# Encoder kernel, Fourier branch of the mixer: the second weight granule formed directly behind the first, ahead of the masked products; the maxima of one half moved behind exponentials

## The chip, the cores and the metric

One core of a Trainium2 chip runs the whole kernel in one launch. The metric is the device time of one execution in microseconds, the median of several runs; lower is better. The engines of the core are named as in the profile: PE (matrix products), PEld (its weight loads), DVE (vector engine), ACT (scalar engine), POOL and SP (here mainly queues that issue DMAs).

## The reference

Two layers of an encoder on 512 tokens of width 1024, in float32. The part that matters is the mixer of each layer:

```python
for l in range(DEPTH):                       # DEPTH = 2
    x = x + 0.5 * swiglu(rms_norm(x, ffn1_norm[l]), ffn1_w_in[l], ffn1_w_out[l])
    x = x + mixer(rms_norm(x, mix_norm[l]), ...)
    x = x + 0.5 * swiglu(rms_norm(x, ffn2_norm[l]), ffn2_w_in[l], ffn2_w_out[l])
return rms_norm(x, final_norm)

def mixer(h, w_in, gate_bias, rpb, w_na_out, w_f_out, w_o):
    z = h @ w_in                             # q, k, v, uf, ga, gf are column blocks of z
    y_na = neighbourhood_attention(q, k, v, rpb) @ w_na_out
    y_f = fourier_mix(uf) @ w_f_out          # real part of a 2-D DFT per channel group
    return (sigmoid(ga + gate_bias[0]) * y_na + sigmoid(gf + gate_bias[1]) * y_f) @ w_o

def neighbourhood_attention(q, k, v, rpb):   # 8 heads of 64, 2-D windows with a learned bias
    s = q k^T * scale + bias, masked outside the window
    return softmax(s) v
```

## The kernel before

**Precision.** A float32 product is made of three PE passes over operands that are each split into a rounded high part and a low rest: high by high, low by high, high by low (`mm3`, lines 316 to 318). So each operand that reaches PE is first split: ACT copies the high part, then DVE subtracts it from the source and writes the low part.

**Weights.** All weights lie in DRAM as granules of 128 x 1024 numbers, in the order of use. `Stream` (`ws`) fetches them ahead by DMAs on SP's queue into `raw` tiles, and prepares them: `Item.prep` writes `whi` on ACT (line 191) and `wlo` on DVE (line 194). `whi` and `wlo` have three buffers each. A second method, `Item.prep_high`, writes `whi` alone (line 171) and gives back a function that writes `wlo` (line 175) where it is called; before, it is used at one place (line 1684), with the low part written at once. `ws.prep(ws.pos + n)` prepares granules up to the n-th that is not yet used.

**The mixer's order.** In `stage_mixer` the order of instructions on PE, DVE and ACT is the order of the Python lines: the block at line 1501 is under `manual_schedule` for these three engines, so each runs its instructions strictly as they are written. SP and POOL are ordered by the scheduler.

**Attention.** Heads go in pairs (`hp` 0 to 3), queries in halves, which gives eight products `p0` to `p7`, two to a head pair. For each, `att_scores` writes two PSUM banks (one per head `e`), and `Probs` does the softmax per `e`: `maxes(e)` adds the bias tile `bm` (the mask is in it) and takes row maxima, two custom DVE instructions and two accumulator reads (line 1295); `exps(e)`, two ACT instructions (line 1304); `inverse(e)`, a DVE reciprocal (line 1307); `scaled(e)`, two ACT instructions (line 1312). Then PE transposes the result (line 1320), ACT copies it to `p` (line 1330), and PE multiplies it by the values (line 1346). The bias tiles have four buffers, two per head pair, so the load for head pair 3 (line 1259, on SP) needs the buffers that `p2` and `p3` read.

**Fourier branch.** Its four channel groups end in split tiles `y`: groups 0 and 1 are `y0`, `y1` and groups 2 and 3 are `w0`, `w1`. The high parts are written by ACT (line 1243), the low parts by DVE when the closure is called (line 1247): `yf += [y0(), y1()]` makes four such DVE instructions, `yf += [w0(), w1()]` four more. The list `yf` is then multiplied by `f_w_out`: `rows_of(yf, tb, first_f)` takes two weight granules, here called A (for groups 0 and 1) and B (for groups 2 and 3), each for six products of 512 columns (lines 316 to 318, shown as `ps<-whi,y` and `ps<-wlo,y`), and `f_copy` (line 1498) moves the sum out on DVE.

**The place of the change** is lines 1583 to 1601. It stands between the scores of `p2` and `p3` and the first `rows_of(yf, 0, first_f)`; meanwhile PE runs the key projection `k3` (24 products). DVE and ACT in that time make the low parts of `w0`, `w1`, the split of granules A and B, and the softmax of `p2` and `p3`. The block runs once in each of the two layers.

Of the kernel before, what the change touches and what calls it, by code (L numbers as in the profile page):

```python
# [91 lines left out]
def encoder_kernel(  # L92
# [19 lines left out]
    def slot(dt=F32, s="k", shape=(4, 256)):  # L112
        return kp.tile([P, *shape], dt, tag="k", name=nm(s), bufs=23)

    def hilo(s):
        t = slot(F32R, s, (2, T))
        return t[:, 0, :], t[:, 1, :]

    def bank(s="ps"):
        return pp.tile([P, T], F32, tag="ps", name=nm(s))  # L120
# [191 lines left out]
    ws = Stream()  # L312
    raw_pool = [None]

    def mm3(ps, lh, ll, rh, rl, start, stop, again=False):
        PE.matmul(ps, lh, rh, start=start, stop=False, skip_group_check=again)  # L316
        PE.matmul(ps, lh, rl, start=False, stop=False, skip_group_check=again)  # L317
        PE.matmul(ps, ll, rh, start=False, stop=stop, skip_group_check=again)  # L318
# [729 lines left out]
    def stage_mixer(l, norm, nxt):  # L1048
        mp = mix_pool[0]

        def tmp(dt=F32, s="x"):
            return mp.tile([P, T], dt, tag="tmp", name=nm(s), bufs=10)
# [20 lines left out]
        def proj_T(scale, ahead=AHEAD, hook=None):  # L1073
            ps = bank()
            wh, wl = ws.next(ahead)
            for kt in range(DT):
                if hook and kt == 5:
                    hook()
                c = slice(kt * P, (kt + 1) * P)
                mm3(ps, wh[:, c], wl[:, c], *xs[kt], kt == 0, kt == DT - 1)  # L1080

            def out(now=True):

                t = tmp(s="q")
                V.tensor_tensor(t, ps, R, ALU.mult)
                hi, lo = hilo("q")

                def high():
                    if scale is None:
                        S.activation(hi, t, AF.Copy)  # L1090
                    else:
                        S.activation(hi, t, AF.Copy, scale=scale)
                    return rest

                def rest():
                    if scale is None:
                        V.tensor_tensor(lo, t, hi.bitcast(F32), ALU.subtract)
                    else:
                        V.scalar_tensor_tensor(lo, t, scale, hi.bitcast(F32), ALU.mult, ALU.subtract)
                    return hi, lo  # L1100

                return high() if now else high

            return out
# [122 lines left out]
        def four_y(p1, qs):  # L1227
            y = tmp(s="fy")
            V.tensor_tensor(y[:, 0:256], p1[:, 0:256], qs[:, 0:256], ALU.subtract)
            V.tensor_copy(y[:, 256:257], p1[:, 256:257])  # L1230
            V.tensor_tensor(y[:, 511:256:-1], p1[:, 1:256], qs[:, 1:256], ALU.add)
            return y
# [6 lines left out]
        def four_high(y):  # L1239
            hi, lo = hilo("y")  # L1240
            hv, lv = [t.rearrange("p (m a z r) -> p m a z r", m=2, a=2, r=8) for t in (hi, lo)]
            for m in range(2):
                S.activation(hv[:, m], by_unit(y, m), AF.Copy)

            def low_of():
                for m in range(2):
                    V.tensor_tensor(lv[:, m], by_unit(y, m), hv[:, m].bitcast(F32), ALU.subtract)
                return hi, lo

            return low_of  # L1250
# [17 lines left out]
        def att_scores(i):  # L1268

            hp, pr = divmod(i, 2)  # L1270
            (qh, ql), (kh, kl) = q[hp], k[hp]
            ps = [bank(), bank()]
            for jj in range(2):
                j = 2 * pr + jj
                qs = slice(j * P, (j + 1) * P)
                for i, (a, b) in enumerate(((qh, kh), (qh, kl), (ql, kh))):
                    for e in range(2):
                        r = slice(64 * e, 64 * e + 64)
                        PE.matmul(
                            ps[e][:, jj * 256 : (jj + 1) * 256], a[r, qs], keys(b[r], j), start=i == 0, stop=i == 2  # L1280
                        )
            return ps
# [193 lines left out]
        yf = []  # L1476
# [24 lines left out]
        with tc.manual_schedule(engines={mybir.EngineType.DVE, mybir.EngineType.Activation}):  # L1501
            with tc.manual_schedule(engines={mybir.EngineType.PE}):
# [69 lines left out]
                w0 = four_y(f0[0], g0)  # L1572
                w1 = four_y(f1[0], g1)
                q3 = q3(False)
                w0 = four_high(w0)
                w1 = four_high(w1)
# [3 lines left out]
                q3 = q3()  # L1580
                p2, p3 = [Probs(i, att_scores(i)) for i in (2, 3)]
                k3 = proj_T(None, 0)
                p2.maxes(0)
                p2.maxes(1)
                ws.prep(ws.pos + 1)
                p2.exps(0)
                p2.exps(1)
                p3.maxes(0)
                p2.inverse(0)
                p3.maxes(1)  # L1590
                p2.inverse(1)
                yf += [w0(), w1()]
                ws.prep(ws.pos + 2)
                p2.scaled(0)
                p2.scaled(1)
                p3.exps(0)
                k[2] = k2()
                p3.inverse(0)
                p3.exps(1)
# [93 lines left out]
        def low(h, src, s):  # L1693
            l_ = slot(F32R, s + "l")
            V.tensor_tensor(l_, src, h.bitcast(F32), ALU.subtract)
            return h, l_, 0
# [141 lines left out]
    for l in range(L):  # L1838
        nxt = Norm(3 * l + 1)
        stage_ffn(norm, nxt, False)  # L1840
        norm, nxt = nxt, Norm(3 * l + 2)
        stage_mixer(l, norm, nxt)
        norm, nxt = nxt, Norm(3 * l + 3)
        stage_ffn(norm, nxt, l == L - 1)
        norm = nxt
# [148 lines left out]
```

## Time and profile before

| | |
|---|---|
| time, median of 3 runs | 1852.29 us (1851.4 to 1854.55) |
| profiled execution | 1856.7 us, of which 1854.9 us are its span |
| PE busy | 1838.5 us, 99% of the span |
| PEld, DVE, ACT busy | 1530.0, 1601.6 and 1312.2 us |
| mean granted PE clock | 0.998 |

The span goes from the first to the last instruction of the profiled execution; what lies around it is the difference to that execution's own time. PE's ends are modelled: a 512-column product is shown with 0.39 us although the next one starts some 0.23 us later, so what PE loses is read from the starts of successive products, not from its busy share. In the rows of the timeline the columns are: start in us from the span's beginning, duration in us, engine, line, operation, what it writes and reads, shape, count, and in brackets the idle time before it and what ended it.

### The profile page before, as it was taken

Reading aid. Unit: us, or ns where it says so; the run is one execution under the profiler, and the core shown is the slowest. Engines: PE = TensorE matmul, PEld = TensorE weight load, DVE = VectorE, ACT = ScalarE, POOL = GpSimd, SP = SyncE. Lnnn points to the kernel's source line nnn. Section 1 sums busy time; section 2 is a strip of 40 time slices with the busy share of each in tenths; the row PEclk is TensorE's granted clock in tenths of the full one; section 3 lists DMA queues with packets and bytes.
Section 4 is the critical chain, followed back from the end, with each engine's and each line's share of the span. In section 5 each row is a group of like instructions: output and inputs, shape, how many; then the busy total and the mean of one; then the engine's idle time right before and its main releaser. Section 6 shows DMA issues by size and latency. Waiting matters only on the chain.

```text
span 1854.9 us, 24564 instructions
## 1 busy us (share of the span) xinstructions
PE 1838.5 (99%) x8850; PEld 1530.0 (82%) x8850; DVE 1601.6 (86%) x1942; ACT 1312.2 (71%) x1777; POOL 173.1 (9%) x212
## 2 busy tenths in 40 slices
PE   9999999999999999999999999999999999999998
PEld 7888888888888888888888888888888888788886
DVE  7878899786989987889998888998869899787898
ACT  6777875668576777777667778665776776677865
POOL 0001010100111010001010100101001111010010
PEclk9999999999999999999999999999999999999999
DMA  9898799934887798979888887988258866989795
GB/s 297 229 231 223 189 275 272 232 103 126 236 234 173 180 221 228 211 198 270 248 197 225 222 218 198 284 288 187 85 181 201 227 174 184 201 225 218 214 282 148
DMA packets 198282, 395.72 MB, mean 213 GB/s; under 512 B 103760, under 2 KB 103888, under 8 KB 198160
## 3 DMA queue, kind: packets, MB, share of 16 engines
q1 hardware_dynamic: 168912, 294.23, 50.4%
q0 software_dynamic: 28816, 99.38, 30.2%
q8 instruction: 69, 1.13, 0.2%
q10 hardware_dynamic: 432, 0.55, 0.1%
q14 instruction: 53, 0.43, 0.1%
HBM read 367.88 MB, written 2.11 MB: 199 GB/s over the span
## 4 chain that ended last, share of the span: by engine, by line
PE 88%; DVE 4%; ACT 3%; DMA 2%; issue 1%; SPq 0%; ACTq 0%; DVEq 0%
PE A L505 9%; PE A L502 9%; PE A L503 9%; PE o L505 7%; PE o L502 7%; PE o L503 7%; PE B L503 5%; PE B L502 5%; PE B L505 5%; PE C L502 2%; PE C L503 2%; PE C L505 2%; PE ps L316 2%; PE ps L317 2%; PE ps L318 2%; DMA zt<-zs 2%
## 5 line engine op out<-in xcount | busy, mean ns | idle before, releaser
L194 DVE TENSOR_TENSOR wlo<-raw,whi 128x1024 fp32r<-128x1024 f32 (+1 forms) x534 | 630.0, 1189 | 183.9 <-ACT whi L191 180.0
L191 ACT ACTIVATE whi<-raw 128x1024 fp32r<-128x1024 f32 (+1 forms) x534 | 545.4, 1033 | 253.4 <-DVE raw L164 53.2
L150 POOL DMA_DIRECT2D raw<-in_wst_dram x166 | 144.3, 889 | 1361.0 <-DMA raw<-in_wst_dram 532.1
L164 DVE TENSOR_TENSOR raw<-raw,raw 128x1024 f32<-128x1024 f32 (+1 forms) x148 | 175.9, 1189 | 2.0
L503 PE MATMUL A<-whi,xl 128*128 128x512 f32 x400 | 155.7, 389 | 0.0
L502 PE MATMUL A<-whi,xh 128*128 128x512 f32 x400 | 155.7, 389 | 0.0
L357 ACT ACTIVATE at<-zt 128x1024 uint16<-128x1024 uint16 (+2 forms) x96 | 110.2, 1166 | 22.9 <-DMA zt<-zs 22.9
L186 ACT ACTIVATE whi<-raw 128x1024 fp32r<-128x1024 f32 (+1 forms) x83 | 85.9, 1037 | 44.0 <-issue 12.5
L505 PE MATMUL A<-wlo,xh 128*128 128x512 f32 x400 | 115.0, 389 | 0.0
L187 DVE SCALAR_TENSOR_TENSOR wlo<-raw,whi 128x1024 fp32r<-128x1024 f32 (+1 forms) x83 | 98.2, 1191 | 12.7 <-ACT whi L186 12.7
L505 PEld LDWEIGHTS A<-wlo,xh 128*128 128x128 f32 x400 | 75.1, 188 | 15.5
L503 PEld LDWEIGHTS A<-whi,xl 128*128 128x128 f32 x400 | 75.1, 188 | 15.4
L502 PEld LDWEIGHTS A<-whi,xh 128*128 128x128 f32 x400 | 75.1, 188 | 15.4
L502 PE MATMUL C<-whi,xh 128*128 128x512 f32 x208 | 81.1, 390 | 0.1
L503 PE MATMUL C<-whi,xl 128*128 128x512 f32 x208 | 81.0, 389 | 0.0
L502 PE MATMUL B<-whi,xh 128*128 128x512 f32 x208 | 81.0, 389 | 0.0
L503 PE MATMUL B<-whi,xl 128*128 128x512 f32 x208 | 81.0, 389 | 0.0
L724 ACT ACTIVATE th<-sn,rh 128x512 f32<-128x512 f32 x80 | 55.1, 716 | 36.1 <-DVE sn L577 35.2
L347 ACT ACTIVATE zs<-th 128x1024 uint16<-128x1024 uint16 x80 | 79.5, 1042 | 1.3 <-DVE th L731 1.3
L572 ACT ACTIVATE sn<-A 128x512 f32<-128x512 f32 x104 | 59.0, 583 | 23.6 <-PE A L505 23.6
L505 PE MATMUL C<-wlo,xh 128*128 128x512 f32 x208 | 59.8, 389 | 0.0
L505 PE MATMUL B<-wlo,xh 128*128 128x512 f32 x208 | 59.8, 389 | 0.0
(428 smaller groups left out, 4678.8 us busy)
## 6 DMA issues: line engine op xcount, KB each, us to landing
raw<-in_wst_dram SPq DMA_DIRECT2D x468, 512.0 KB, 5.9
raw<-in_wst_dram POOLq DMA_DIRECT2D x176, 512.0 KB, 7.9
bm<-in_bias_dram SPq DMA_DIRECT2D x16, 512.0 KB, 4.4
raw<-in_wst_dram SPq DMA_DIRECT2D x30, 256.0 KB, 4.5
x<-in_xin_dram SPq DMA_DIRECT2D x4, 512.0 KB, 10.2
raw<-in_wst_dram POOLq DMA_DIRECT2D x8, 256.0 KB, 8.6
dft<-in_dft_dram POOLq DMA_DIRECT2D x8, 256.0 KB, 11.0
gb<-in_gbias_dram SPq DMA_DIRECT2D x4, 512.0 KB, 9.1
```

What stands on the lines that cost most here:

```text
L150: G.dma_start(out=self.t, in_=wst[GRAN_AT[self.plus]][:, 0 : self.n], accum_op=ALU.add)
L164: V.tensor_tensor(self.raw.t, self.raw.t, self.add.t, ALU.add)
L186: S.activation(hi, t, AF.Copy, scale=-1.0)
L187: self.last = V.scalar_tensor_tensor(lo, t, -1.0, hi.bitcast(F32), ALU.mult, ALU.subtract)
L191: S.activation(hi[:, cs], t[:, cs], AF.Copy)
L194: self.last = V.tensor_tensor(lo[:, cs], t[:, cs], hi[:, cs].bitcast(F32), ALU.subtract)
L347: S.activation(s[:, h], words[:, h], AF.Copy)
L357: S.activation(to[:, w], t[:, w], AF.Copy)
L502: PE.matmul(ps, lh, rh, start=start, stop=False, skip_group_check=again)
L503: PE.matmul(ps, ll, rh, start=False, stop=False, skip_group_check=again)
L505: PE.matmul(ps, lh, rl, start=False, stop=stop, skip_group_check=again)
L572: S.activation(t[:, b, :], ps[b], AF.Copy)
```

## The change

Five edits in one block of straight code in `stage_mixer`, run in both layers:

```diff
                 k3 = proj_T(None, 0)
+                yf += [w0(), w1()]
                 p2.maxes(0)
                 p2.maxes(1)
                 ws.prep(ws.pos + 1)
+                low = ws.prep_high()
                 p2.exps(0)
                 p2.exps(1)
+                p2.inverse(0)
                 p3.maxes(0)
-                p2.inverse(0)
-                p3.maxes(1)
                 p2.inverse(1)
-                yf += [w0(), w1()]
-                ws.prep(ws.pos + 2)
+                low()
                 p2.scaled(0)
                 p2.scaled(1)
                 p3.exps(0)
+                p3.maxes(1)
                 k[2] = k2()
                 p3.inverse(0)
                 p3.exps(1)
```

No instruction is added or removed. PE's order is the same as before.

On DVE, layer 1, the first piece of the difference between the two orders: the Fourier lows (`y`, line 1247) and the start of `p2`'s maxima (line 1295).

```order
 L1247 TENSOR_TENSOR y_3597<-fy_3558,y_3597 128x256 x2
 L1247 TENSOR_TENSOR y_3600<-fy_3563,y_3600 128x256 x2
+L1247 TENSOR_TENSOR y_3705<-fy_3694,y_3705 128x256 x2
+L1247 TENSOR_TENSOR y_3708<-fy_3698,y_3708 128x256 x2
 L1295 ISA s_3756,nmx_3758<-ps_3742,bm_3526 128x256
 L1295 ISA nmx_3758 128x1
```

The lows of `w0` and `w1` (3705 and 3708) now stand ahead of `p2`'s maxima.

Further down on DVE, from `p3`'s maxima on (`nmx_3777` is `p3`; `rs_3760` the reciprocal of `p2`; `wlo_3828` before and `wlo_3818` now are the low part of granule B).

```order
 L1295 ISA nmx_3777 128x1
 L1307 RECIPROCAL rs_3760<-sm_3759 128x2
+L175 TENSOR_TENSOR wlo_3818<-raw_3349,whi_3817 128x1024
 L1295 ISA s_3776,nmx_3777<-ps_3762,bm_3528 128x256
 L1295 ISA nmx_3777 128x1
 L1295 ISA s_3776,nmx_3777<-ps_3762,bm_3528 128x256
 L1295 ISA nmx_3777 128x1
-L1307 RECIPROCAL rs_3760<-sm_3759 128x2
-L1247 TENSOR_TENSOR y_3705<-fy_3694,y_3705 128x256 x2
-L1247 TENSOR_TENSOR y_3708<-fy_3698,y_3708 128x256 x2
-L194 TENSOR_TENSOR wlo_3828<-raw_3349,whi_3827 128x1024
 L1097 TENSOR_TENSOR q_3635<-q_3633,q_3635 128x512
```

The low part of B has moved ahead of the maxima of `p3`'s second head (`s_3776`), and the second reciprocal of `p2` ahead of both.

On ACT, at the same place: the high parts of granules A (3809 before, 3813 now) and B (3827 before, 3817 now) and `p2`'s exponentials (line 1304).

```order
-L191 ACTIVATE whi_3809<-raw_3232 128x1024
+L191 ACTIVATE whi_3813<-raw_3232 128x1024
+L171 ACTIVATE whi_3817<-raw_3349 128x1024
 L1304 ACTIVATE s_3756,sm_3759<-s_3756,nmx_3758 128x256 x2
 L1304 ACTIVATE s_3757,sm_3759<-s_3757,nmx_3758 128x256 x2
-L191 ACTIVATE whi_3827<-raw_3349 128x1024
 L1312 ACTIVATE s_3756<-s_3756,rs_3760 128x256 x2
 L1312 ACTIVATE s_3757<-s_3757,rs_3760 128x256 x2
```

The high part of B has moved from behind the four exponentials of `p2` to ahead of them. SP's queue has the same order as before; its load of the bias tiles for head pair 3 still waits for `p3`'s maxima, which now stand elsewhere.

## The prediction

> **What bounds the kernel now.** I read the page first, then PE's view of the chain of waits, then the timeline of the block that is changed, in both layers. The page's first part, and of the view of what PE waits for the one row that lies in the changed block:
>
> ```profile
> span 1854.9 us, 24564 instructions
> PE 1838.5 (99%) x8850; PEld 1530.0 (82%) x8850; DVE 1601.6 (86%) x1942; ACT 1312.2 (71%) x1777; POOL 173.1 (9%) x212
> PE ps L317 <- DVE wlo L194: 2.1, 2, 1.0
> ```
>
> PE sets the end: it is busy for 99% of the span and idle for 1854.9 - 1838.5 = 16.4 us in all. So only what shortens an idle time of PE can make the kernel faster, and there is little to shorten. The last row is the place of the change: two waits (one per layer) for a `wlo` written at L194, by a product of line 317. The timeline of layer 2 shows it, first PE and the DVE instructions ahead of it:
>
> ```profile
> 1342.91 0.39 PE L316 MATMUL ps<-whi,y 128*128 128x512 f32 x1
> 1344.28 0.39 PE L316 MATMUL ps<-whi,y 128*128 128x512 f32 x1
> 1344.43 1.21 DVE L194 TENSOR_TENSOR wlo<-raw,whi 128x1024 fp32r<-128x1024 f32 x1
> 1345.57 0.68 DVE L1097 TENSOR_TENSOR q<-q,q 128x512 fp32r<-128x512 f32 x1
> 1345.69 0.50 PE L317 MATMUL ps<-wlo,y 128*128 128x512 f32 x1 [1.03 <-DVE wlo L194]
> 1346.03 0.39 PE L318 MATMUL ps<-whi,y 128*128 128x512 f32 x1
> ```
>
> From 1342.91 to 1344.28 PE starts six products, one every 0.228 us. At that pace the product that reads B's low part would start at 1344.51 and the one behind it at 1344.74. They start at 1345.69 and 1346.03, so PE loses 1346.03 - 1344.74 = 1.29 us. B's low part ends at 1344.43 + 1.21 = 1345.64; PE's steady pace is back as if the product had started 0.16 us after that (1346.03 - 0.228 = 1345.80). Layer 1 shows the same pattern at the same place:
>
> ```profile
> 426.14 0.39 PE L316 MATMUL ps<-whi,y 128*128 128x512 f32 x1
> 427.56 0.50 PE L317 MATMUL ps<-wlo,y 128*128 128x512 f32 x1 [1.04 <-DVE wlo L194]
> 427.90 0.40 PE L318 MATMUL ps<-whi,y 128*128 128x512 f32 x1
> ```
>
> Here the loss is 427.90 - (426.14 + 2 x 0.228) = 1.30 us. Both together are 2.59 us, 0.14% of the time. That is the most that this block can give.
>
> **The change part by part.** I rebuild DVE's time from the starts in layer 2, because the length of a row overlaps the next instruction.
>
> ```profile
> 1335.50 2.18 DVE L1247 TENSOR_TENSOR y<-fy,y 128x256 fp32r<-128x256 f32 x4
> 1337.59 0.41 DVE L1295 CUSTOM_DVE_ANT_0 s<-ps,bm 128x256 f32<-128x256 f32 x1
> 1339.65 1.23 DVE L194 TENSOR_TENSOR wlo<-raw,whi 128x1024 fp32r<-128x1024 f32 x1 [0.60 <-ACT whi L191]
> 1340.79 0.42 DVE L1295 CUSTOM_DVE_ANT_0 s<-ps,bm 128x256 f32<-128x256 f32 x1
> 1341.48 0.16 DVE L1307 RECIPROCAL rs<-sm 128x2 f32<-128x2 f32 x1
> 1341.56 0.40 DVE L1295 CUSTOM_DVE_ANT_0 s<-ps,bm 128x256 f32<-128x256 f32 x1
> 1342.31 2.20 DVE L1247 TENSOR_TENSOR y<-fy,y 128x256 fp32r<-128x256 f32 x4
> ```
>
> A granule's low part takes 1340.79 - 1339.65 = 1.14 us of DVE, two maxima 1341.48 - 1340.79 = 0.69, a reciprocal 0.08, four Fourier lows 1344.43 - 1342.31 = 2.12. In the new order the four lows of `w0`, `w1` start at 1337.59 (their high parts come from the same ACT row as before, see below) and end at 1339.71; `p2`'s four maxima take 1.38, to 1341.09; A's low part to 1342.23; a reciprocal to 1342.31; `p3`'s first two maxima to 1343.00; a reciprocal to 1343.08. B's low part then starts at 1343.08 instead of 1344.43: 1.35 us earlier. Of that, 0.69 is the two maxima that now stand behind it, and 0.60 is the idle time in front of A's low part, which the moved Fourier lows fill; nothing else on DVE becomes shorter. B's low part ends at 1343.08 + 1.21 = 1344.29, and PE's product could run as from 1344.29 + 0.16 = 1344.45. It is due at 1344.51. So the wait goes, with 0.06 us to spare. My sum can be off by some 0.2 us (a dozen pieces, each read to 0.01 to 0.02), so between 0 and 0.15 us per layer may stay. I take 0 to 0.1 and write a gain of 1.25 per layer, 2.5 in all.
>
> This holds only if ACT feeds DVE in time. ACT's rows:
>
> ```profile
> 1333.90 2.32 ACT L1243 ACTIVATE y<-fy 128x256 fp32r<-128x256 f32 x4 [1.46 <-DVE fy L1231]
> 1338.56 1.06 ACT L191 ACTIVATE whi<-raw 128x1024 fp32r<-128x1024 f32 x1
> 1339.50 0.51 ACT L1304 ACTIVATE s<-s,nmx 128x256 f32<-128x256 f32 x1
> 1341.47 1.05 ACT L191 ACTIVATE whi<-raw 128x1024 fp32r<-128x1024 f32 x1
> 1342.43 1.70 ACT L1312 ACTIVATE s<-s,rs 128x256 f32<-128x256 f32 x4
> 1344.02 0.50 ACT L1304 ACTIVATE s<-s,nmx 128x256 f32<-128x256 f32 x1
> 1346.35 1.71 ACT L1312 ACTIVATE s<-s,rs 128x256 f32<-128x256 f32 x4 [0.26 <-DVE rs L1307]
> ```
>
> The high parts of `w0`, `w1` are done at 1336.22, before DVE wants them. B's high part (0.96 us of ACT) now runs from 1339.50 to 1340.46, long before DVE reads it. The four exponentials of `p2` (1.97 us) follow from 1340.46; their first maxima are there at 1339.71 + 0.42 = 1340.13. They end at 1342.43, so `scaled` starts at 1342.43 as before: the high part and the exponentials have changed places on ACT and nothing behind them moves. `p3`'s exponentials start at 1344.02 as before, the second pair at 1345.00; its maxima now end at 1344.22 + 0.42 = 1344.64 and 1344.99, just in time. The two reciprocals that stand ahead of B's low part wait for exponentials that end at 1341.44 and 1342.43, and DVE reaches them at 1342.23 and 1343.00, so they hold nothing up. Should they, every microsecond goes straight to PE.
>
> What is late next on PE, once it is 1.29 us ahead? The transposes, and then the products that read `p`:
>
> ```profile
> 1346.95 1.04 PE L1320 MATMUL ps<-ident,s 128*128 128x128 f32 x8
> 1350.60 1.03 PE L1320 MATMUL ps<-ident,s 128*128 128x128 f32 x8
> ```
>
> The first needs `p2` scaled, done at 1342.43 + 1.70 = 1344.13; it would start at 1345.66. The second needs `p3` scaled, done at 1346.35 + 1.71 = 1348.06 or a little earlier; it would start at 1349.31. Both keep over 1.2 us. After them ACT and DVE work behind PE, so they move with it.
>
> On SP the load of the bias for head pair 3 needs `p3`'s maxima, and weights queue behind it:
>
> ```profile
> 1341.59 1.08 SPq L1259 DMA_DIRECT2D bm<-in_bias_dram  x2
> 1342.77 5.16 SPq L148 DMA_DIRECT2D raw<-in_wst_dram  x3
> 1347.60 0.33 SPq L148 DMA_DIRECT2D raw<-in_wst_dram  x1
> 447.18 0.42 DVE L1295 CUSTOM_DVE_ANT_0 s<-ps,bm 128x256 f32<-128x256 f32 x1 [0.46 <-PE ps L1279]
> bm<-in_bias_dram SPq DMA_DIRECT2D x16, 512.0 KB, 4.4
> ```
>
> `p3`'s last maximum ends at about 1344.99 instead of 1342.3, so the second bias load, and two of the three weight loads behind it, are issued 2.7 us later; the third goes at 1347.60 in any case. The first reader of that bias is, in layer 1, at 447.18, which is 23 us after the load's place there (426.14 is the same moment as 1344.28 here, so 1342.3 is 424.2). The load lands in 4.4 us. With 2.7 us more and PE 1.3 us earlier there remain over 14 us, so I cost this at nothing; without that cover it would cost up to 2.7 us.
>
> **Against which time.** The profiled execution took 1856.7 us, 4.4 more than the median 1852.29. That excess has its own place, PE's longest wait:
>
> ```profile
> 1604.92 0.61 PE L505 MATMUL C<-wlo,xh 128*128 128x512 f32 x2
> 1604.29 1.36 ACT L357 ACTIVATE at<-zt 128x1024 uint16<-128x1024 uint16 x1 [4.92 <-DMA zt<-zs]
> 1608.27 0.50 PE L502 MATMUL A<-whi,t7h 128*128 128x512 f32 x1 [2.73 <-ACT whi L191]
> 1609.50:1612.90 3.40, 3.40 (x9) 2.63 (x8) 3.40 (x5) 2.27 (x4) 0.21 (x1) 0.50 1.03 370
> 1612.90:1616.30 3.40, 3.40 (x16) 2.77 (x15) 2.69 (x4) 3.40 (x4) 1.50 (x2) 1.00 0.76 213
> ```
>
> A transposing DMA (`zt`) landed late, ACT waited 4.92 us for it, and PE, due at 1605.38, went on at 1608.27: 2.89 us. Then the granted clock stood at 0.50 for 3.4 us, in which 9 products were begun against 16 in the next 3.4 us: 7 x 0.228 = 1.6 us. Together 4.5 us, which takes 1856.7 to 1852.2, the median. So the common execution has no such event, and the gain is taken from the median: 1852.29 - 2.5 = 1849.8 us.
>
> [...]
>
> **The rivals.** First, that the gain is given back: PE arrives 1.3 us earlier at something which is not timed by PE, most likely weights for the gates, whose loads are among those now issued later. The 100 us behind the block in either layer, with PE's busy time first behind the length, and the DMA share next to last:
>
> ```profile
> 428.00:528.00 100.00, 100.00 (x593) 83.67 (x592) 80.52 (x120) 70.52 (x122) 8.58 (x10) 1.00 0.68 187
> 1346.10:1446.10 100.00, 100.00 (x593) 83.68 (x592) 80.55 (x120) 70.50 (x122) 8.60 (x10) 1.00 0.69 188
> ```
>
> For this rival speaks that DMA is at 0.68; against it that PE is never idle there, so every feed has some reserve, though a busy share doesn't tell how much. The time would be 1852.3.
>
> Second, that the change does not do what it says: a reciprocal ahead of B's low part catches DVE waiting for ACT. It needs `p2`'s exponentials 0.6 us later than I find, and 1.9 us later for the whole gain to go. The time would be 1852.3 there, and slower beyond it; nothing in the rows delays ACT so much.
>
> Third, slower: the shifted work of layer 2 meets the transposing DMAs of its second feed-forward block in another phase, so that the event at 1605 comes in the common execution. Its price is 4.5 us: once 1849.8 + 4.5 = 1854.3, twice 1858.8. It decides as soon as it comes in more than half of the executions. For it speaks that it came once in the execution shown; against it that all streams behind the change move together, so their phase to each other stays.
>
> **How the numbers follow.** A measurement of this kernel can tell some 0.2%, 3.7 us, from no change. The forecast, the wait gone in both layers and the gain kept, gets 0.74; given back 0.10; not as said 0.05; the late transpose 0.11. The forecast of 1849.8 lies only 1.2 us inside the bound of 1848.6; the three runs of before spread over 3.15 us, so a median can well fall 1.2 us off, and a bit more may come from small waits of a tenth or two that the view does not list. I give 0.30 of the 0.74 to faster by over 0.2% and 0.44 to within it. The rivals of 1852.3 are within (0.15). The third gives 0.03 to within (once) and 0.08 to slower. So faster 0.30, same 0.62, slower 0.08. The range reaches from 1847.0 (forecast and 2.8 us of spread) to 1853.0 (given back and 0.7 of spread); outside lie most of the third rival and the tails. The forecast's own range is 1848.3 to 1851.3.
>
> **What would show it.** Right: in both layers no wait of line 317 for the `wlo` of granule B (now written at L175 of that kernel's numbering), B's low part starting 1.3 to 1.4 us earlier relative to PE's products and at once behind a reciprocal, no idle time in front of A's low part, and `p2`'s scaling at the same place. Wrong: an idle time of DVE in front of a reciprocal, a new wait of PE at the transposes or at the first products of the gates, or a bias tile that lands after its reader is due.

## The result and the profile after

The changed kernel takes 1849.11 us (median of 22 runs, 1845.71 to 1851.6), before 1852.22 us over as many runs. The ratio is 0.9982, 95% interval 0.9976 to 0.9988: 3.3 us faster, between 2.2 and 4.4. So it is faster, by less than the 0.2% that was set as the bound. The forecast was 1849.8 us, 2.5 us faster. Here and below, the ratio and its interval are an estimate from all runs and not the quotient of the two medians, and a gain in us is worked out from the ratio. One of the eleven runs of the kernel called the dose, below, took 3098.84 us at a mean granted clock of 0.556; it is left out of that kernel's time and ratio.

The page's first part of the kernel after, and the whole view of what PE waits for:

```profile
span 1848.9 us, 24562 instructions
PE 1836.9 (99%) x8850; PEld 1528.5 (83%) x8850; DVE 1601.9 (87%) x1942; ACT 1312.6 (71%) x1777; POOL 173.2 (9%) x212
PE ps L136 <- DVE ones L132: 1.2, 1, 1.2
PE o L505 <- DVE wlo L194: 0.9, 2, 0.7
PE cl L502 <- ACT whi L191: 0.6, 1, 0.6
PE o L502 <- ACT whi L191: 0.4, 1, 0.4
PE cl L505 <- DVE wlo L194: 0.3, 1, 0.3
```

The row `PE ps L317 <- DVE wlo` (2.1 us, twice) is gone, and none for the new line 175 has come in its place. The number of instructions on each engine that the page lists is the same as before; the two by which the totals differ are of the kinds that the page doesn't count as busy. The two profiled executions differ by 6.0 us in span, more than the change is worth: the one before held the late transposing DMA, which this one doesn't. PE's idle time falls from 16.4 to 1848.9 - 1836.9 = 12.0 us, its busy time by 1.6 us, as much as the half-clock stretch of the profile before was reckoned to cost.

The block in the timeline of layer 2 after, in order of time:

```profile
1335.39 4.33 DVE L1247 TENSOR_TENSOR y<-fy,y 128x256 fp32r<-128x256 f32 x8
1339.39 1.06 ACT L171 ACTIVATE whi<-raw 128x1024 fp32r<-128x1024 f32 x1
1340.34 0.51 ACT L1304 ACTIVATE s<-s,nmx 128x256 f32<-128x256 f32 x1
1341.00 1.23 DVE L194 TENSOR_TENSOR wlo<-raw,whi 128x1024 fp32r<-128x1024 f32 x1
1342.34 1.71 ACT L1312 ACTIVATE s<-s,rs 128x256 f32<-128x256 f32 x4
1342.79 0.39 PE L316 MATMUL ps<-whi,y 128*128 128x512 f32 x1
1342.88 0.17 DVE L1307 RECIPROCAL rs<-sm 128x2 f32<-128x2 f32 x1
1342.96 1.22 DVE L175 TENSOR_TENSOR wlo<-raw,whi 128x1024 fp32r<-128x1024 f32 x1
1344.15 0.40 PE L316 MATMUL ps<-whi,y 128*128 128x512 f32 x1
1344.39 0.40 PE L317 MATMUL ps<-wlo,y 128*128 128x512 f32 x1
1344.62 0.39 PE L318 MATMUL ps<-whi,y 128*128 128x512 f32 x1
1345.54 1.03 PE L1320 MATMUL ps<-ident,s 128*128 128x128 f32 x8
```

The reader sees eight Fourier lows in one row, A's low part (1341.00) without idle time in front of it, B's low part at once behind the reciprocal, and PE going on at its own pace: from 1344.15 two steps of 0.228 us lead to 1344.61, and the product is there at 1344.62. Layer 1 shows the same:

```profile
426.81 0.40 PE L316 MATMUL ps<-whi,y 128*128 128x512 f32 x1
427.04 0.40 PE L317 MATMUL ps<-wlo,y 128*128 128x512 f32 x1
427.28 0.39 PE L318 MATMUL ps<-whi,y 128*128 128x512 f32 x1
```

### The profile page after: what moved, and what is told of

Read it like the earlier page. It is cut to its first block, busy times and chain, and to the rows that moved or that the text cites. A ratio compares the mean times of both kernels' runs of the same rounds, so it can differ in the third digit from the quotient of the medians.

```text
span 1848.9 us, 24562 instructions
## 1 busy us (share of the span) xinstructions
PE 1836.9 (99%) x8850; PEld 1528.5 (83%) x8850; DVE 1601.9 (87%) x1942; ACT 1312.6 (71%) x1777; POOL 173.2 (9%) x212
## 4 chain that ended last, share of the span: by engine, by line
PE 91%; DVE 4%; issue 2%; DMA 2%; ACT 1%; POOL 0%; SPq 0%; DVEq 0%; ACTq 0%; POOLq 0%
PE A L502 10%; PE A L505 10%; PE A L503 10%; PE o L505 6%; PE o L502 6%; PE o L503 6%; PE B L502 5%; PE B L503 5%; PE B L505 5%; PE ps L316 4%; PE ps L317 3%; PE ps L318 3%; PE C L503 2%; PE C L502 2%; PE C L505 2%
```

## The experiments

Each kernel's loss of PE at B's low part is read as in the prediction: the start of the product behind the waiting one, less the start of the product before it, less two steps of 0.228 us. Before, this is 1.30 + 1.29 = 2.59 us for the two layers; after, 0.03 together. The first four experiments are compared with 33 runs of the kernel before, median 1852.28 us; the last three ran on another chip and are compared with 21 runs of it there, median 1851.45 us.

**The Fourier lows alone.**

```diff
+                yf += [w0(), w1()]
                 p2.maxes(0)
...
-                yf += [w0(), w1()]
                 ws.prep(ws.pos + 2)
```

> One part alone: the lows of w0, w1 stand ahead of p2's maxima, the rest as before. Theory (time follows PE's loss at B's low part): the idle time in front of A's low part is filled, B's low part starts about 0.66 us earlier, PE loses about 0.63 us per layer instead of 1.29, in all 1.3 us less than before: 1850.9 us. Rival (the gain comes from the loads on SP that wait for p3's last maximum and are issued later): that maximum ends 1.4 us later here, half of what it is in the whole change, so half of 3.1 us too, but with PE's loss in this block unrelated to it.

Measured 1850.58 us, ratio 0.9991 (0.9983 to 1.0000). Layer 2 of its timeline:

```profile
1343.26 1.22 DVE L194 TENSOR_TENSOR wlo<-raw,whi 128x1024 fp32r<-128x1024 f32 x1
1343.77 0.39 PE L316 MATMUL ps<-whi,y 128*128 128x512 f32 x1
1344.54 0.50 PE L317 MATMUL ps<-wlo,y 128*128 128x512 f32 x1 [0.38 <-DVE wlo L194]
1344.87 0.40 PE L318 MATMUL ps<-whi,y 128*128 128x512 f32 x1
```

PE loses 1344.87 - 1343.77 - 0.456 = 0.64 us (0.62 in layer 1), as the sum gave. Half the wait goes with this edit. Theory and rival forecast nearly the same time here, so it is the rows, not the time, that speak for the theory.

**The maxima alone.**

```diff
                 p3.maxes(0)
                 p2.inverse(0)
-                p3.maxes(1)
                 p2.inverse(1)
...
                 p3.exps(0)
+                p3.maxes(1)
```

> One part alone: the maxima of p3's second head stand behind its first exponentials and behind B's low part, the rest as before, B's high part behind p2's exponentials included. Theory: B's low part starts about 0.66 us earlier (the two maxima of 0.69 us are gone from in front of it), PE loses about 0.63 us per layer, 1.3 us less than before: 1850.9 us. Rival (loads on SP): the bias load waits as long as in the whole change, so the whole gain of 3.1 us: 1849.1 us.

Measured 1849.53 us, ratio 0.9992 (0.9983 to 1.0001). The bias load of head pair 3 is drawn out here (its two DMAs, with the waiting in between, cover 4.51 us, against 1.08 before and 2.22 in the change), and yet PE still waits:

```profile
1339.74 4.51 SPq L1259 DMA_DIRECT2D bm<-in_bias_dram  x2
1342.40 0.39 PE L316 MATMUL ps<-whi,y 128*128 128x512 f32 x1
1343.25 0.50 PE L317 MATMUL ps<-wlo,y 128*128 128x512 f32 x1 [0.46 <-DVE wlo L194]
1343.59 0.40 PE L318 MATMUL ps<-whi,y 128*128 128x512 f32 x1
```

PE loses 0.73 us (0.71 in layer 1), 0.1 more than expected. The medians differ by 2.75 us, the ratio gives 1.5: seven of the eleven runs take 1848.2 to 1850.3 us, the other four 1852.1 to 1854.1. The time's interval holds both half the gain and just the whole; the loss of PE is what tells.

**All but the Fourier lows.**

```diff
-                yf += [w0(), w1()]
                 p2.maxes(0)
...
                 p2.inverse(1)
+                yf += [w0(), w1()]
                 low()
```

> The whole change without its first edit: the lows of w0, w1 stand directly ahead of B's low part again. B's high part is ahead of p2's exponentials, so these end about 1 us later than before, and the first reciprocal, now ahead of p3's maxima, holds DVE until they are there. Theory: DVE idles about 0.7 us at that reciprocal and again at the second, B's low part starts near 0.2 to 0.3 us later than before, PE loses about 1.5 to 1.6 us per layer: 0.5 us slower than before, 1852.8 us. Rival (what counts is that B's split is formed directly behind A's): most of the gain stays, 1850 us.

Measured 1851.86 us, ratio 1.0000 (0.9991 to 1.0009). DVE, PE and SP in layer 2:

```profile
1338.82 1.23 DVE L194 TENSOR_TENSOR wlo<-raw,whi 128x1024 fp32r<-128x1024 f32 x1 [0.59 <-ACT whi L191]
1340.74 0.17 DVE L1307 RECIPROCAL rs<-sm 128x2 f32<-128x2 f32 x1 [0.69 <-ACT s L1304]
1341.66 4.52 SPq L1259 DMA_DIRECT2D bm<-in_bias_dram  x2
1343.43 0.39 PE L316 MATMUL ps<-whi,y 128*128 128x512 f32 x1
1345.19 0.50 PE L317 MATMUL ps<-wlo,y 128*128 128x512 f32 x1 [1.38 <-DVE wlo L175]
1345.53 0.39 PE L318 MATMUL ps<-whi,y 128*128 128x512 f32 x1
```

The second rival of the prediction is real here: the reciprocal holds DVE for 0.69 us, since the exponentials now stand behind B's high part. PE loses 1.64 us (1.65 in layer 1), more than before, and the time shows no gain (1852.8 was expected; the interval is 1.7 us to either side). A second hold of about 0.7 us, at the next reciprocal, was expected too and did not come. So forming B's high part directly behind A's brings nothing while the Fourier lows stay where they were, although the maxima are moved here as well; and the bias load, drawn out in this kernel as well, brings none either. From the maxima alone this kernel differs by the early high part and by the place of `p2`'s first reciprocal; which share of the 3.29 - 1.44 = 1.85 us between them is due to which was not run.

**All but the early high part.** `low = ws.prep_high()` and `low()` are taken out, and B is prepared in one go where `low()` stood:

```diff
-                low = ws.prep_high()
...
-                low()
+                ws.prep(ws.pos + 2)
```

> The whole change without its second edit: B's high part stands behind p2's exponentials again, its low part and everything else as in the change. Theory: the exponentials start about 0.25 us earlier, the high part ends about 1343.3 on the scale of the profile before, B's low part waits 0.1 to 0.2 us for it, PE loses 0.1 to 0.2 us per layer: 1849.3 us, not to be told from the change. Rival (the early high part carries the gain): back to 1852.2 us.

Measured 1849.74 us, ratio 0.9987 (0.9978 to 0.9995).

```profile
1340.67 1.04 ACT L191 ACTIVATE whi<-raw 128x1024 fp32r<-128x1024 f32 x1
1341.75 1.23 DVE L194 TENSOR_TENSOR wlo<-raw,whi 128x1024 fp32r<-128x1024 f32 x1
1342.74 0.39 PE L316 MATMUL ps<-whi,y 128*128 128x512 f32 x1
1343.37 0.40 PE L318 MATMUL ps<-whi,y 128*128 128x512 f32 x1
```

B's low part starts when its high part ends, 1341.71. PE loses 0.17 us (0.18 in layer 1), too little for the view of waits to list it. So with everything else in place, the early high part is worth some 0.3 us of the 2.6; the Fourier lows and the maxima, each taken alone above, make the rest.

**A dose of the wait.** `low()` moved behind `q[3] = q3()`:

```diff
-                low()
...
                 q[3] = q3()
+                low()
```

> The whole change, but B's low part is formed later on DVE, behind the low part of q3: a dose of the suspected wait. Theory (PE's local loss is the time, one to one): on the scale of the profile before, DVE reaches B's low part at 1345.8 (the first reciprocal of p3 waits for exponentials that end at 1345.1), PE loses 2.6 us per layer, 1.3 more than before: 1852.2 + 2.7 = 1854.9 us. Rival (later work absorbs or gives back what PE loses or gains here): clearly less than 2.7 us slower. If a wait of this length halves the granted clock for 3.4 us, as it did once in the profile before, 1.6 us more per layer: 1858.1 us.

Measured 1855.7 us (median of ten runs), ratio 1.0022 (1.0013 to 1.0031).

```profile
1346.51 0.39 PE L316 MATMUL ps<-whi,y 128*128 128x512 f32 x1
1349.37 0.50 PE L317 MATMUL ps<-wlo,y 128*128 128x512 f32 x1 [2.47 <-DVE wlo L175]
1349.71 0.39 PE L318 MATMUL ps<-whi,y 128*128 128x512 f32 x1
```

PE loses 2.74 us in layer 2, and layer 1 waits as long (2.48 us in its row): 5.5 in all, 2.9 more than before. The time is 4.1 us longer, with an interval of 2.4 to 5.7 that holds 2.9. Nothing absorbs it. In the profiled execution the clock stays at full speed behind both waits: the products directly behind them start 0.23 us apart (428.71 to 429.42 and 1349.71 to 1350.40), and the granted clock is 1.00 in the 3.4 us from 430.95 and from 1351.85. In others it may not have: the mean granted clock is 0.999 in two of the ten runs, which take 1853.2 and 1855.0 us, and 0.998 or 0.997 in eight, which take 1856.5 us on average; 3.4 us at half clock lower the mean by 0.001 (3.4 x 0.5 of 1853 us). That this makes the rest of the 4.1 us is an inference, because only one of the ten has a trace.

**A larger dose.** `low()` one step later still, behind `k3 = k3(False)`:

```diff
-                low()
...
                 k3 = k3(False)
+                low()
```

> As the late one, with B's low part one step later still, behind the vector step of k3. Theory: DVE reaches it at 1346.8, PE loses 3.7 us per layer, 2.4 more than before: 1852.2 + 4.7 = 1856.9 us with the clock at full speed. With the clock at 0.50 for 3.4 us behind each wait 1860.1 us. Rival (given back or absorbed): clearly less than 4.7 us slower.

Measured 1858.33 us, ratio 1.0034 (1.0021 to 1.0047). The wait in either layer, the products before and behind it in layer 2, and the 3.4 us behind it (with PE's busy time and instructions first behind the length, and the granted clock third from the end):

```profile
429.91 0.50 PE L317 MATMUL ps<-wlo,y 128*128 128x512 f32 x1 [3.45 <-DVE wlo L175]
1347.02 0.39 PE L316 MATMUL ps<-whi,y 128*128 128x512 f32 x1
1350.85 0.50 PE L317 MATMUL ps<-wlo,y 128*128 128x512 f32 x1 [3.44 <-DVE wlo L175]
1351.18 0.39 PE L318 MATMUL ps<-whi,y 128*128 128x512 f32 x1
430.95:434.35 3.40, 3.40 (x14) 2.91 (x13) 0.69 (x1) 1.65 (x3) 0.00 (x0) 0.50 0.85 306
1351.85:1355.25 3.40, 3.40 (x20) 2.89 (x19) 0.69 (x1) 1.61 (x3) 0.00 (x0) 1.00 0.84 296
```

PE loses 3.7 us per layer, 4.8 more than before in all. Behind the first wait the clock is halved for 3.4 us, which is up to 1.7 us more (3.4 x 0.5); behind the second it isn't. 4.8 + 1.7 = 6.5; measured 6.3, with an interval of 3.9 to 8.7, between the two expectations (4.7 without and 7.9 with a halved stretch behind each wait). How often the clock is halved in the executions without a trace isn't known.

**An earlier low part.** `low()` directly behind `low = ws.prep_high()`:

```diff
                 low = ws.prep_high()
+                low()
...
-                low()
```

> The whole change, but B's low part stands directly behind A's, ahead of both reciprocals and of p3's maxima: it ends 0.85 us earlier. Theory (what can be had here is had): PE loses nothing at B's low part, as in the change; p2's scaling starts 1.1 us later and still ends before PE's transposes want it, by 0.3 us, p3's by 0.2 us: 1849.1 us. Rival (the change leaves a rest of the wait, which the profile doesn't show): faster than the change. If the margins at the transposes are used up, slower than the change by a few tenths.

Measured 1848.54 us, ratio 0.9983 (0.9974 to 0.9992), the same gain as the change's within the intervals. Only in this kernel does B's low part stand directly behind A's; in the change it is the high parts that follow each other directly, and two reciprocals and two maxima lie between the low parts.

```profile
1341.20 1.23 DVE L175 TENSOR_TENSOR wlo<-raw,whi 128x1024 fp32r<-128x1024 f32 x1
1342.54 1.71 ACT L1312 ACTIVATE s<-s,rs 128x256 f32<-128x256 f32 x4 [1.06 <-DVE rs L1307]
1343.23 0.39 PE L316 MATMUL ps<-whi,y 128*128 128x512 f32 x1
1343.68 0.39 PE L318 MATMUL ps<-whi,y 128*128 128x512 f32 x1
1344.59 1.03 PE L1320 MATMUL ps<-ident,s 128*128 128x128 f32 x8
```

ACT now waits 1.06 us for the reciprocal, scaling ends at 1344.25, 0.34 us ahead of the transposes, and PE loses nothing (1343.68 - 1343.23 = 0.45). The place is empty: a wider margin buys no time.

PE's loss and the time together, against before:

| kernel | PE's loss, two layers (us) | less that of before | time against before (us, 95%) |
|---|---|---|---|
| the change | 0.03 | -2.6 | -3.3 (-4.4 to -2.2) |
| Fourier lows alone | 1.26 | -1.3 | -1.7 (-3.1 to 0.0) |
| maxima alone | 1.44 | -1.1 | -1.5 (-3.1 to +0.2) |
| all but the lows | 3.29 | +0.7 | 0.0 (-1.7 to +1.7) |
| all but the early high part | 0.35 | -2.2 | -2.4 (-4.1 to -0.9) |
| dose | 5.5 | +2.9 | +4.1 (+2.4 to +5.7) |
| larger dose | 7.4 | +4.8, and 1.7 for the clock once | +6.3 (+3.9 to +8.7) |
| earlier low part | 0 | -2.6 | -3.1 (-4.8 to -1.5) |

Every loss lies in its interval of the time. In the six kernels without a dose the time is 0.2 to 0.7 us lower than the loss says, each within its interval but all to the same side. Four of them share one set of runs of the kernel before, so this may be that set; it may also be a small gain elsewhere.

## Why the prediction was right

**The bound.** PE's loss at one place was said to be the time. Eight kernels, from no loss to 7.4 us, agree with that, within intervals of 1.1 to 2.4 us to either side; a difference of half a microsecond between loss and time could not be seen.

**DVE's sum.** The block stands 0.12 us earlier in the profile after (1342.79 against 1342.91), so B's low part was forecast for 1343.08 - 0.12 = 1342.96. It starts at 1342.96. A's low part was forecast for 1340.97 and starts at 1341.00. The two sources of the 1.35 us, the idle time filled and the two maxima put behind, were each taken alone: 1.33 and 1.15 us less of PE's loss over the two layers. As named they make 0.60 + 0.69 = 1.29, not 1.35. The row's idle time of 0.60 counts from the end of the last accumulator read (1339.05); reckoned by starts, like the rest of the sum, it is 0.68, and the two maxima are 0.67 (1341.56 to 1342.23). The sum itself was right.

**What was left of the wait.** I allowed 0 to 0.1 us per layer; it is under 0.02. By the prediction's own reckoning with 0.16 us, the product could have run 0.04 us before it was due (1342.96 + 1.22 + 0.16 = 1344.34, due at 1344.38), where 0.06 was forecast and the sum was given an error of 0.2: that nothing at all was left of the wait is in part luck. The gain by PE's loss is thus 2.56 us, the forecast 2.5, the measured 3.3 with an interval from 2.2. Whether the time gained more than the wait, or the median of runs only fell so, isn't settled; no row shows a further source.

**ACT.** The exponentials start at 1340.34, forecast 1340.46 - 0.12. Scaling starts at 1342.34, forecast 1342.31. The high part and the exponentials did change places at no cost.

**What comes next on PE.** The first transposes start at 1345.54 (forecast 1345.66 - 0.12), scaling has ended at 1344.05: 1.5 us of reserve, as said.

**SP.** The bias and the weights behind it are issued later (in layer 1 the bias from 425.66 instead of 423.46), and PE has no wait for a load in the 45 us behind the block in either layer. In layer 1:

```profile
425.66 2.22 SPq L1259 DMA_DIRECT2D bm<-in_bias_dram  x2
427.97 1.85 SPq L148 DMA_DIRECT2D raw<-in_wst_dram  x3
446.50 0.42 DVE L1295 CUSTOM_DVE_ANT_0 s<-ps,bm 128x256 f32<-128x256 f32 x1 [0.46 <-PE ps L1279]
```

The load has gone out by 427.9, its reader comes at 446.50 and waits for PE alone.

**The rivals.** Given back: no; the gain's interval begins at 2.2 us, and the losses of the two doses are not smaller in the time than at the place. The held reciprocal: not in the change, but it is what happens as soon as the Fourier lows stay behind. The late transposing DMA: neither the profile after nor one of the seven experiments' has it in PE's waits; one execution each does not say how rare it is. That it accounts for the 4.4 us by which the profiled execution before exceeded the median is argued, not shown.

## What to carry to other kernels

Where one engine is busy throughout, read its loss from the starts of successive instructions, and rebuild the other engines' order from start-to-start times of the profile before: here that placed the moved instructions of the change to within 0.03 us, and B's low part in the experiments to within 0.1 us. When a producer is to be ready earlier, look at what fills its engine just before: a waiting gap that other due work can fill (0.68 us here), and work that can stand behind because its own reader is later (0.67 us), were the gain; the reordering of the producer's first half was worth some 0.3 us of the 2.6. It can even cost, as in the kernel without the moved Fourier lows: there a reciprocal, ahead of B's low part in the same queue, waited 0.69 us for the work that the early half had displaced.

## What the runs showed of the hardware

Equal waits of PE, 3.45 and 3.44 us in one execution of the larger dose, were followed once by 3.4 us at half clock and once by none; a wait of 2.73 us in the profile before was followed by it, two of 2.48 and 2.47 us in the dose were not. So no length of the wait between 2.5 and 3.5 us decided by itself here.

What else may have decided is an estimate, worked out from the times at which the granted clock changes. In the profile before it falls to 0.50 at 1609.48, is back at full speed at 1612.89, 3.413 us later, and falls next at 1851.83, after the last product. From 1612.89 to 1851.83 are 238.93 us, 70 times 3.4133 us. The record of the granted clock begins 1604.26 us ahead of the first fall there, and in the profile after 1839.78 us ahead of the only one, at 1844.33: 470 and 539 times the same. If the changes within an execution so lie on a grid of 3.4133 us, it can be counted on to each wait.

In the larger dose the granted clock is 1.00 from 427.50 to 430.90 and 0.50 from 430.95 to 434.35, so a stretch of 3.413 us begins there at 430.94. With a wait reckoned from the moment at which PE's next product is due, the cell of such a grid just ahead of the halved stretch holds 2.20 us of the wait in the profile before (1606.07 to 1608.27) and 2.38 us in the larger dose (427.53 to 429.91). The other wait of the larger dose is split by the grid at 1349.13, into 1.88 and 1.72 us. Near the two waits of the dose the clock doesn't change, so where they lie is not shown. By this estimate a wait was followed by the halved clock in the two cases where 2.2 us or more of it fell into one cell, and not in the one where it was 1.9 us or less. A wait as long as the halved stretch was not needed: 2.73 us came before one of 3.413 us.

That the place on the grid decided is thus an estimate from two waits with the halved clock behind them and one without; no run varied it alone.
